# A hybrid decoder layer in float32: where the odd heads' values come back from DRAM, which pool the gates' blocks live in, and which engine multiplies in the gate

## The chip, the core and the metric

The kernel runs on one core of one Trainium2 chip. The engines of a core work side by side: PE (TensorE) multiplies matrices out of on-chip memory (SBUF) into eight accumulator banks (PSUM), ACT (ScalarE) applies functions and copies, DVE (VectorE) does elementwise arithmetic, POOL (GpSimd) and SP (SyncE) here only issue transfers (DMAs). The metric is the device time of one execution in microseconds (us); the median of three runs of the kernel before is 1163.79 us (1162.83 to 1166.5).

## The reference

One layer on 512 tokens, model width 1024, all in float32. What matters here, with the feed-forward part left out:

```python
rq, rk, rv, rg, cq, ckv, krope, gr, gm = jnp.split(rms_norm(x) @ w_in, offsets, axis=-1)
ro = retention(rope(rq), rope(rk), rv)             # 4 heads, q/k width 256, v width 512
a_ret = (rms_norm(ro) * jax.nn.silu(rg)) @ w_br    # head by head, 512 rows of w_br each
a_mla = causal_block_attention(q, k, v) @ w_bm     # 8 heads of latent attention
mixed = jax.nn.sigmoid(gr) * a_ret + jax.nn.sigmoid(gm) * a_mla
x = x + mixed @ w_o
x = x + jnp.square(jax.nn.relu(rms_norm(x) @ w_up)) @ w_down
x = x + jax.nn.sigmoid(rms_norm(x) @ w_ple_gate) * (p @ w_ple)
```

Silu is z times sigmoid(z).

## The kernel before

**Arithmetic.** Activations lie transposed, channels on the 128 partitions and the 512 tokens along the free dimension. Each float32 product is made of three matmuls on a high and a low part of both factors (`mm3`: low by high, high by low, high by high). ACT makes the high part (`wh_...` of a weight), DVE subtracts it from the raw tile for the low part (`wl_...`). A matmul group therefore waits for a chain: DMA, ACT copy, DVE subtraction.

**Products of 2 by 2 blocks in seven parts.** The projections `rv` (values, two heads at a time), `rg` (a head's gate), `br` (a head's rows of w_br) and `dn` (w_down) are each cut into 2 by 2 blocks and made of seven smaller products p = 1, 7, 2, 6, 5, 4, 3. For p = 7, 6 and 4 the weight is a sum of blocks, built in one raw tile: SP loads the first block, and POOL adds the others by accumulating DMAs (L222), for p = 7 at once, for p = 6 only after DVE has taken p = 7's low part out of the tile, for p = 4 only after p = 6's. The raw tile of head h is called `wr_rg{h}70` at all three. The results are joined by `seven_out` (L736): ACT copies p = 1, 7 and 6 out of PSUM into z_11, z_22 and z_21 (L741), DVE adds p = 2, 5 and 4 to them (L746), and p = 3 leaves block 12 in PSUM. PSUM tiles are shared: p = 6 accumulates in the tile of p = 1, so it waits until ACT has copied z_11 away.

**A retention head** h, in PE's order: `ret_qk` (rq, rk), for even h `ret_v` (the values of heads h and h+1), `ret_gate` for p = 1 and 7, `ret_scores` (rs: scores times decay, split into ath and atl), `ret_gate` for p = 2 and 6, `ret_attend` (ro: four groups of 12 matmuls, one for each 128 value channels, and every group goes through all four tiles of values rv{h}0 to rv{h}3), then `ret_gate` for p = 5, 4, 3. The values of the odd heads are stored to DRAM by POOL when they are made (`aside`, L353: v00d to v03d for head 1, v10d to v13d for head 3) and loaded again by SP just before their head (`odd_v`, L779); ACT and DVE split each into rv{h}{j}h and rv{h}{j}l. The gate takes a sigmoid on ACT (L849) and a multiplication by z on DVE (L852). The branch product `br` of head h is done among the next head's rq and rk.

**After the heads**, `ret_turn` (tr) transposes the summed branch for channel block n, `mix` multiplies it by the gate (L943) and adds the attention branch `ze{n}` (L944), and splits it into mix{n}h and mix{n}l. `out_part` starts the first two blocks of the output product `wo` with mix0 to mix3, `out_proj` does the rest.

**Order.** A table of steps (from L1225) is walked at build time. It gives the order of the loads and the order of PE's instructions, which is kept. On ACT, DVE, POOL and SP a list scheduler orders the instructions by its own cost estimates and by the free slots of the tile pools, and each engine then runs its list strictly in that order: an instruction that waits holds up all behind it. The pools that matter: `dyn` with 47 slots for tiles of 128 by 512 (`T`), `keep` with 16 (`K`), six raw weight tiles, three pairs of `wh` and `wl`.

## Time and profile before

| what | us |
|---|---|
| median of three runs (lowest, highest) | 1163.79 (1162.83, 1166.5) |
| the profiled execution: device time | 1163.55 |
| its span, first to last instruction | 1161.8 |
| PE busy | 1110.2 (96%) |
| DVE busy | 783.7 (67%) |
| ACT busy | 548.5 (47%) |
| POOL busy | 85.9 (7%) |
| PE idle, span less busy | 51.6 |
| mean granted PE clock | 0.985 of full |

A row of a timeline reads: start, duration, engine, line, operation, what is written from what is read, partitions by elements, count; in brackets the time the engine stood idle before it, and what ended the wait. A row of issued DMAs reads: destination and source, issuing queue, count, KB each, median us from issue to landing. PE's stages in us of the span, by the first matmuls of each: inputs and attention up to 239.8, its branch product (bm) from there, the retention heads from 283.4, the transposes (tr) from 706.4, the output product (wo) from 715.3, feed-forward (up, dn) from 767.3, embedding (pg) to the end.

### The profile page before, as it was taken

What the parts mean: (1) busy time and instruction counts of PE and PEld (TensorE: products, weight loads), DVE (VectorE), ACT (ScalarE), POOL (GpSimd) and SP (SyncE); (2) the same over time, 40 slices, a digit from 0 to 9 for tenths busy, and PEclk for the clock granted to TensorE, in tenths of its full rate; (3) what the DMA queues carried; (4) which work ended last, traced back from release to release, by engine and by line L of the source; (5) the groups of instructions that cost most, each with busy time, mean ns of one, the idle gap of its engine ahead of it and who ended that gap; (6) DMA issues with size and microseconds to landing.
All of it is one profiled execution on the core that took longest, in us unless ns stands there. A gap on an engine that the chain in (4) does not pass through costs nothing.

```text
span 1161.8 us, 14724 instructions
## 1 busy us (share of the span) xinstructions
PE 1110.2 (96%) x5517; PEld 937.3 (81%) x5517; DVE 783.7 (67%) x1258; ACT 548.5 (47%) x774; POOL 85.9 (7%) x113
## 2 busy tenths in 40 slices
PE   9999989999999989899999698999999999999998
PEld 7878878888889879677878686878888888888877
DVE  7877676557766857866587489554656567567675
ACT  7447556444455535344533453333544344444542
POOL 0000000001120010012000000000100100101000
PEclk9999999999999999999999899999999999999999
DMA  7132222367796774489548663576656755747511
GB/s 258 65 108 88 78 74 64 129 223 221 192 275 163 179 192 113 106 205 259 158 113 201 164 181 111 180 216 200 140 158 191 160 158 179 175 137 193 160 37 73
DMA packets 59799, 182.26 MB, mean 157 GB/s; under 512 B 7312, under 2 KB 8720, under 8 KB 59472
## 3 DMA queue, kind: packets, MB, share of 16 engines
q1 hardware_dynamic: 45744, 131.75, 33.7%
q0 software_dynamic: 13840, 49.55, 22.3%
q8 instruction: 43, 0.70, 0.2%
q14 instruction: 28, 0.23, 0.1%
q10 hardware_dynamic: 144, 0.03, 0.0%
HBM read 167.41 MB, written 11.80 MB: 154 GB/s over the span
## 4 chain that ended last, share of the span: by engine, by line
PE 49%; DMA 7%; DVE 4%; issue 2%; ACT 1%; POOL 0%; SPq 0%; ACTq 0%; POOLq 0%; DVEq 0%
PE up L167 15%; PE dn L167 13%; PE pg L167 4%; PE wo L167 3%; PE rg L167 3%; PE br L167 2%; PE rk L167 2%; DMA wr_rg<-wstream 2%; DMA wr_br<-wstream 2%; PE ro L167 2%; PE gr L167 1%; DMA wr_rv<-wstream 1%; PE rq L167 1%; PE pw L167 1%; DMA v13d<-cv 1%
## 5 line engine op out<-in xcount | busy, mean ns | idle before, releaser
L167 PE MATMUL dn<-wh_dn,cl 128*128 128x512 f32 x224 | 87.2, 389 | 0.0
L167 PE MATMUL dn<-wh_dn,ch 128*128 128x512 f32 x224 | 87.1, 389 | 0.0
L167 PE MATMUL dn<-wl_dn,ch 128*128 128x512 f32 x224 | 87.1, 389 | 0.0
L260 ACT ACTIVATE wh_dn<-wr_dn 128x1024 fp32r<-128x1024 f32 x32 | 34.0, 1063 | 75.7 <-PE up L167 54.3
L260 ACT ACTIVATE wh_up<-wr_up 128x1024 fp32r<-128x1024 f32 x32 | 34.0, 1061 | 58.7 <-PE up L167 29.3
L264 DVE TENSOR_TENSOR wl_dn<-wr_dn,wh_dn 128x1024 fp32r<-128x1024 f32 x32 | 39.1, 1221 | 27.5 <-ACT wh_dn L260 27.5
L260 ACT ACTIVATE wh_rg<-wr_rg 128x1024 fp32r<-128x1024 f32 x28 | 29.4, 1056 | 48.0 <-DMA wr_rg<-wstream 32.8
L264 DVE TENSOR_TENSOR wl_up<-wr_up,wh_up 128x1024 fp32r<-128x1024 f32 x32 | 39.1, 1223 | 18.2 <-ACT wh_up L260 17.9
L1016 DVE SCALAR_TENSOR_TENSOR f<-up,bcx 128x512 f32<-128x512 f32 x32 | 20.6, 686 | 44.1 <-PE up L167 44.1
L167 PEld LDWEIGHTS dn<-wh_dn,cl 128*128 128x128 f32 x224 | 42.1, 188 | 8.8
L167 PEld LDWEIGHTS dn<-wh_dn,ch 128*128 128x128 f32 x224 | 42.1, 188 | 8.7
L167 PEld LDWEIGHTS dn<-wl_dn,ch 128*128 128x128 f32 x224 | 42.1, 188 | 8.6
L260 ACT ACTIVATE wh_rv<-wr_rv 128x1024 fp32r<-128x1024 f32 x28 | 29.6, 1060 | 37.7 <-PE rv L167 11.6
L260 ACT ACTIVATE wh_dn<-dr_dn 128x1024 fp32r<-128x1024 f32 x24 | 25.5, 1061 | 42.5 <-PE up L167 29.4
L264 DVE TENSOR_TENSOR wl_dn<-dr_dn,wh_dn 128x1024 fp32r<-128x1024 f32 x24 | 29.3, 1223 | 22.4 <-ACT wh_dn L260 22.4
L222 POOL DMA_DIRECT2D dr_dn<-wstream x24 | 21.4, 893 | 279.1 <-DMA dr_dn<-wstream 166.0
L260 ACT ACTIVATE wh_br<-wr_br 128x1024 fp32r<-128x1024 f32 x28 | 29.6, 1059 | 25.8 <-DMA wr_br<-wstream 8.9
L264 DVE TENSOR_TENSOR wl_rg<-wr_rg,wh_rg 128x1024 fp32r<-128x1024 f32 x20 | 24.2, 1223 | 25.7 <-ACT wh_rg L260 25.4
L264 DVE TENSOR_TENSOR wl_rv<-wr_rv,wh_rv 128x1024 fp32r<-128x1024 f32 x20 | 24.4, 1224 | 17.4 <-ACT wh_rv L260 15.9
L1074 DVE TENSOR_TENSOR d<-d,dn 128x1024 f32<-128x1024 f32 x24 | 29.3, 1220 | 6.4 <-PE dn L167 6.4
L643 ACT ACTIVATE p<-p,ng,hr 128x128 f32<-128x128 f32 (+3 forms) x32 | 20.6, 647 | 14.9 <-DVE ng L641 14.9
L222 POOL DMA_DIRECT2D wr_br<-wstream x16 | 14.2, 887 | 174.6 <-DVE wl_br L264 53.3
(1917 smaller groups left out, 3669.5 us busy)
## 6 DMA issues: line engine op xcount, KB each, us to landing
wr_up<-wstream SPq DMA_DIRECT2D x32, 512.0 KB, 4.4
wr_dn<-wstream SPq DMA_DIRECT2D x32, 512.0 KB, 3.5
dr_dn<-wstream POOLq DMA_DIRECT2D x24, 512.0 KB, 8.3
wr_rv<-wstream SPq DMA_DIRECT2D x20, 512.0 KB, 4.9
wr_rg<-wstream SPq DMA_DIRECT2D x20, 512.0 KB, 4.7
wr_br<-wstream SPq DMA_DIRECT2D x20, 512.0 KB, 4.9
wr_rv<-wstream POOLq DMA_DIRECT2D x16, 512.0 KB, 7.2
wr_rg<-wstream POOLq DMA_DIRECT2D x16, 512.0 KB, 6.8
```

The costliest lines, as they stand in the source:

```text
L167: return tc.keep_in_program_order(nc.tensor.matmul(*a, **k))
L222: nc.gpsimd.dma_start(raw, chunk(("w", blk, kb, fb, c)), accum_op=ALU.add)
L260: i = ACT(hi, raw, AF.Copy, scale=sign)
L264: TT(lo, raw, hi.bitcast(F32), op=ALU.subtract)
L643: ACT(cols[b], cols[b], AF.Exp, bias=ng[:, b:b + 1], scale=d["rq"][:, b], accum_out=sums[:, b:b + 1])
L1016: STT(u[:, i], ps[:, i], 0.0, V["bcx2"], op0=ALU.max, op1=ALU.mult)
L1074: TT(to, to, dps[p], op=ALU.add if sign > 0 else ALU.subtract)
```

## The change

It has seven parts. (1) `odd_v`'s loads are issued by POOL instead of SP, and the steps move behind `ret_scores`; the low part is written into the loaded tile itself, so a value takes two slots and not three. (2) The gate's p = 7 moves behind `ret_scores`: the gate goes 1, scores, 7, 2, 6. (3) A new ring of four slots `Z` holds the gate's z blocks, the finished `zm` and the half-wise `gr` on their way to DRAM, and block 22 of the values; `dyn` goes from 47 slots to 43. (4) ACT applies Silu in place on z, so the sigmoid tile and DVE's multiplication are gone. (5) Head 0's branch sums `ret` go into the `keep` pool and two other spare tiles, all but one pair. (6) Before the output product, the transposes and mixes of blocks 4 and 5 come behind the first half of wo 0, those of blocks 6 and 7 behind the first half of wo 1; before, all four came ahead of both. (7) In the tail, a broadcast uses the second half of a statistics bank instead of a bank of its own.

```diff
-NDYN, NKEEP, NW, NRAW, NDRAW, AHEAD, PREP, EARLY, PAD = 47, 16, 3, 6, 4, 1, 3, 5, 72
+NDYN, NKEEP, NW, NRAW, NDRAW, AHEAD, PREP, EARLY, PAD = 43, 16, 3, 6, 4, 1, 3, 5, 72
...
+    def Z(name):
+        return dyn.tile([P, S], F32, tag="z", name=name, bufs=4)
...
-            t = T(f"zm{n}")
+            t = Z(f"zm{n}")
...
-            c[to] = T(f"{name}{to}")
+            c[to] = (Z if name[0] == "z" or to == 22 else T)(f"{name}{to}")
...
-            t = T(f"cv{h}{j}")
-            nc.sync.dma_start(t, R[h]["v"][j])
-            R[h]["v"][j] = split(t, f"rv{h}{j}")
+            t = T(f"cv{h}{j}", F32R)
+            nc.gpsimd.dma_start(t.bitcast(F32), R[h]["v"][j])
+            R[h]["v"][j] = split(t.bitcast(F32), f"rv{h}{j}", lo=t)
...
-            sg = T(f"sg{h}{blk}")
-            tc.keep_in_program_order(ACT(sg, z, AF.Sigmoid))
             if blk == 12:
-                d["z"][12] = T(f"z{h}_12")
-            TT(d["z"][blk], z, sg, op=ALU.mult)
+                d["z"][12] = Z(f"z{h}_12")
+            tc.keep_in_program_order(ACT(d["z"][blk], z, AF.Silu))
...
-                ret[b, n] = T(f"ret{b}{n}")
+                if p == 3:
+                    ret[b, n] = keep.tile([P, S], F32, tag=("sum", "bc")[i], name=f"ret{b}{n}", bufs=1)
+                else:
+                    ret[b, n] = (K if p in (1, 7) else T)(f"ret{b}{n}")
...
-        t = T(f"gr{n}")
+        t = (T if half is None else Z)(f"gr{n}")
...
-        pb = bcast(PP("pb" + name)[:, 0], lambda b: V["r" + name][:, b:b + 1])
+        pb = bcast(V["st" + name][:, 1], lambda b: V["r" + name][:, b:b + 1])
...
-        if h % 2:
-            step(None, odd_v, h)
...
-        for p in (1, 7):
-            step(("sw", ("rg", h), p, 0), ret_gate, h, p)
+        step(("sw", ("rg", h), 1, 0), ret_gate, h, 1)
         step(None, ret_scores, h)
-        for p in (2, 6):
+        if h % 2:
+            step(None, odd_v, h)
+        for p in (7, 2, 6):
             step(("sw", ("rg", h), p, 0), ret_gate, h, p)
...
-    for n in range(4, 8):
-        step(None, ret_turn, n)
-        step(None, mix, n)
     for n in range(2):
         step(("o", n), out_part, n, 0)
+        for m in (4 + 2 * n, 5 + 2 * n):
+            step(None, ret_turn, m)
+            step(None, mix, m)
```

The scheduler then places the instructions of four engines anew. Three places follow; of the rows' line numbers, those of the change are a few higher (L226 is the accumulating DMA, L264 the weight's high part, L268 its low part, L745 the z copy).

**Head 3's gate, POOL's queue.** Of `wr_rg370` the first row shown is the accumulation for p = 6, the second that for p = 4. Before:

```order
L222 DMA wr_rg350_6040<-wstream 128x1024
L222 DMA wr_rg370_5943<-wstream 128x1024
L222 DMA wr_br370_6345<-wstream 128x1024
L222 DMA wr_rg370_5943<-wstream 128x1024
L222 DMA wr_br350_6505<-wstream 128x1024
```

Now:

```order
L226 DMA wr_rg370_5915<-wstream 128x1024
L226 DMA wr_br370_6307<-wstream 128x1024
L784 DMA cv30_6030<-v10d_5238 128x512
L226 DMA wr_rg370_5915<-wstream 128x1024
L784 DMA cv31_6035<-v11d_5242 128x512
L784 DMA cv32_6040<-v12d_5148 128x512
L784 DMA cv33_6045<-v13d_5151 128x512
L226 DMA wr_br350_6465<-wstream 128x1024
```

One value's load stands ahead of the accumulation for p = 4, three behind it; in head 1 it is two ahead and two behind.

**The same place on ACT** (`z_..<-rg` are the copies out of PSUM, `ath` the splits of the scores, `wh_rg_..<-wr_rg_5943` and `..5915` the weights of p = 6 and p = 4 from the shared tile). Before:

```order
L305 ACTIVATE rv32h<-cv_5992 128x512
L305 ACTIVATE rv33h<-cv_5998 128x512
L260 ACTIVATE wh_rg_6251<-wr_rg_5943 128x1024
L741 ACTIVATE z_11_6034<-rg_6009 128x512
L741 ACTIVATE z_22_6068<-rg_6043 128x512
L305 ACTIVATE ath<-s_6079 128x512
L305 ACTIVATE ath<-s_6090 128x384
L305 ACTIVATE ath<-s_6101 128x256
```

Now:

```order
L264 ACTIVATE wh_rg_6050<-wr_rg_5936 128x1024
L745 ACTIVATE z_11_5982<-rg_5957 128x512
L309 ACTIVATE ath<-s_5993 128x512
L309 ACTIVATE ath<-s_6004 128x384
L264 ACTIVATE wh_rg_6084<-wr_rg_5915 128x1024
```

```order
L264 ACTIVATE wh_rg_6116<-wr_rg_6054 128x1024
L309 ACTIVATE rv30h<-cv_6030 128x512
L264 ACTIVATE wh_rg_6217<-wr_rg_5915 128x1024
L855 ACTIVATE z_11_5982<-z_11_5982 128x512
L309 ACTIVATE rv31h<-cv_6035 128x512
L745 ACTIVATE z_21_6146<-rg_5957 128x512
L264 ACTIVATE wh_rg_6269<-wr_rg_6120 128x1024
L309 ACTIVATE rv32h<-cv_6040 128x512
L309 ACTIVATE rv33h<-cv_6045 128x512
```

Before, the z copies came behind the values and behind p = 4's weight. Now z_11 comes ahead of both p = 6's and p = 4's weight, and the splits of three of the four values come behind p = 4's weight.

**The output product, DVE** (`ge` and `gr` are the gates that become mix4 to mix7, `wl_o` low parts of w_o). Before:

```order
L943 TENSOR_TENSOR gr_6533<-tr_6751,gr_6533 128x512
L306 TENSOR_TENSOR mix4l<-ge_6408,mix4h 128x512
L944 TENSOR_TENSOR gr_6533<-gr_6533,ze_6412 128x512
L306 TENSOR_TENSOR mix5l<-gr_6445,mix5h 128x512
L943 TENSOR_TENSOR gr_6726<-tr_6762,gr_6726 128x512
L306 TENSOR_TENSOR mix6l<-gr_6533,mix6h 128x512
L944 TENSOR_TENSOR gr_6726<-gr_6726,ze_6414 128x512
L264 TENSOR_TENSOR wl_o_6776<-wr_o_6773,wh_o_6775 128x1024
L306 TENSOR_TENSOR mix7l<-gr_6726,mix7h 128x512
```

Now:

```order
L951 TENSOR_TENSOR ge_6364<-ge_6364,ze_6362 128x512
L268 TENSOR_TENSOR wl_o_6691<-wr_o_6688,wh_o_6690 128x1024
L310 TENSOR_TENSOR mix3l<-ge_6364,mix3h 128x512
L268 TENSOR_TENSOR wl_o_6733<-wr_o_6730,wh_o_6732 128x1024
L950 TENSOR_TENSOR ge_6368<-tr_6707,ge_6368 128x512
L950 TENSOR_TENSOR gr_6405<-tr_6719,gr_6405 128x512
```

The second and third `wl_o` stand ahead of everything that mix4 to mix7 need, the second ahead of mix3's low part too.

**The attention's first pair of heads, DVE** (`ha`, `hr`, `nt` are the steps to the heads' normalising factor, which PE's broadcast `pbk` reads; `tra`, `trk` a table of angles for the retention heads). Before:

```order
L604 TENSOR_TENSOR hr<-hr,f_464 128x16
L605 TENSOR_SCALAR nsc<-hr 128x8
L264 TENSOR_TENSOR wl_kq_1034<-wr_kq_1031,wh_kq_1033 128x640
L678 TENSOR_TENSOR zm_946<-gm_915,rbc 128x512
L468 TENSOR_SCALAR tra<-posf,cst 128x512
L264 TENSOR_TENSOR wl_gm_0_1069<-wr_gm_0_1066,wh_gm_0_1068 128x512
L469 TENSOR_SCALAR trk<-tra 128x512
```

Now:

```order
L474 TENSOR_SCALAR trk<-trk 128x512
L328 TENSOR_SCALAR hr<-ha 128x16
L481 SCALAR_TENSOR_TENSOR tra<-trk,tra 128x512
L329 TENSOR_SCALAR hr<-hr 128x16
L481 SCALAR_TENSOR_TENSOR tra<-trk,tra 128x512
L331 TENSOR_TENSOR nt_895<-hr 128x16
L481 SCALAR_TENSOR_TENSOR tra<-trk,tra 128x512
L332 SCALAR_TENSOR_TENSOR nt_895<-nt_895,ha 128x16
L481 SCALAR_TENSOR_TENSOR tra<-trk,tra 128x512
```

The angles were made behind `hr`; now they are made between its steps.

Elsewhere POOL has 125 instructions for 117, SP 333 for 341, DVE 1244 for 1260, ACT two more, both loads of a function table; PE's instructions are the same in kind and number.

4 lines of the change are left out of this document (3 added, 1 removed).

## The prediction

> **What bounds the kernel now.** I read the busy times of the page first, then who waited for whom on PE, then the stages, then the timelines at the long waits.
>
> ```profile
> PE 1110.2 (96%) x5517; PEld 937.3 (81%) x5517; DVE 783.7 (67%) x1258; ACT 548.5 (47%) x774; POOL 85.9 (7%) x113
> ```
>
> PE is the bound, and its work does not change. Only its idle time, 1161.8 of span less 1110.2, 51.6 us, and what it loses to a slower clock can move. The waits of PE, with their sum, count and longest:
>
> ```profile
> PE rg L167 <- ACT z L741: 17.4, 3, 9.9
> PE rk L167 <- DVE wl_rk L264: 5.8, 2, 3.1
> PE wo L167 <- DVE wl_o L264: 4.6, 1, 4.6
> PE pbk L167 <- DVE hr L604: 3.1, 2, 2.3
> ```
>
> The first and the third are what the change touches. Two stretches (length, then busy time and count of PE, PEld, DVE, ACT, POOL, then the granted clock) show that a long wait costs more than itself:
>
> ```profile
> 420.00:440.00 20.00, 13.61 (x92) 13.15 (x92) 9.49 (x14) 7.58 (x12) 1.72 (x2) 0.85 0.76 200
> ...
> 630.00:660.00 30.00, 20.05 (x134) 18.95 (x135) 14.54 (x21) 10.40 (x18) 2.61 (x3) 0.83 0.68 170
> ```
>
> The clock is 0.85 and 0.83 around the two longest waits, where its mean over the span is 0.985. The waits themselves, in heads 1 and 3, at p = 6 of the gate, and the shorter one of head 2:
>
> ```profile
> 436.50 0.58 PE L167 MATMUL rg<-s60h,wl_rg 128*128 128x256 f32 x1 [6.39 <-ACT z L741]
> 652.79 0.58 PE L167 MATMUL rg<-s60h,wl_rg 128*128 128x256 f32 x1 [9.88 <-ACT z L741]
> 560.97 0.38 PE L167 MATMUL rg<-s60h,wl_rg 128*128 128x256 f32 x1 [1.17 <-ACT z L741]
> ```
>
> ACT's z copies are late because ACT goes in order and is stuck on something else. Head 1, then head 3, each with the last copy of ro:
>
> ```profile
> 433.87 0.63 ACT L305 ACTIVATE rv12h<-cv 128x512 fp32r<-128x512 f32 x1 [7.30 <-DMA cv<-v02d]
> ...
> 449.30 0.69 ACT L819 ACTIVATE og<-ro,gn 128x512 f32<-128x512 f32 x1 [0.75 <-PE ro L167]
> ...
> 651.20 1.06 ACT L260 ACTIVATE wh_rg<-wr_rg 128x1024 fp32r<-128x1024 f32 x1 [7.70 <-DMA wr_rg<-wstream]
> 652.16 1.07 ACT L741 ACTIVATE z<-rg 128x512 f32<-128x512 f32 x2
> ...
> 661.72 0.69 ACT L819 ACTIVATE og<-ro,gn 128x512 f32<-128x512 f32 x1 [0.75 <-PE ro L167]
> 665.58 0.69 ACT L819 ACTIVATE og<-ro,gn 128x512 f32<-128x512 f32 x1 [0.75 <-PE ro L167]
> ```
>
> In head 1 it is a value's load, in head 3 the weight of p = 4. The last two rows give the length of ro: two groups end 3.86 us apart, so a group takes 1.93 us. ACT waits for the last group and takes it at once, so ro ends at 449.3 and 665.5.
>
> **The gate's p = 6.** Now z_11 stands ahead of everything slow, so p = 6 starts when PE gets there: 436.50 - 6.39 = 430.1 and 652.79 - 9.88 = 642.9. Both waits go as such. Next late are the values. Ro comes right behind p = 6 in PE's order, each of its groups reads all four values, and the last ones are loaded by POOL behind the accumulation for p = 4. POOL's issues (head 0, where two value stores stand right behind an accumulation, then the accumulations for p = 4 in heads 1 and 3), and times from issue to landing:
>
> ```profile
> 345.37 0.88 POOL L222 DMA_DIRECT2D wr_rg<-wstream  x1 [4.86 <-DVE wl_rg L264]
> 345.94 0.88 POOL L353 DMA_DIRECT2D v00d<-cv  x1
> 346.51 0.88 POOL L353 DMA_DIRECT2D v01d<-cv  x1
> ...
> 426.65 0.86 POOL L222 DMA_DIRECT2D wr_rg<-wstream  x1 [7.95 <-DVE wl_rg L264]
> ...
> 643.89 0.89 POOL L222 DMA_DIRECT2D wr_rg<-wstream  x1 [1.94 <-issue]
> ```
>
> ```profile
> wr_rg<-wstream POOLq DMA_DIRECT2D x1, 512.0 KB, 6.8
> v00d<-cv POOLq DMA_DIRECT2D x1, 256.0 KB, 7.6
> v01d<-cv POOLq DMA_DIRECT2D x1, 256.0 KB, 8.2
> wr_rg<-wstream POOLq DMA_DIRECT2D x1, 512.0 KB, 5.6
> v11d<-cv POOLq DMA_DIRECT2D x1, 256.0 KB, 2.3
> ```
>
> The first three land at 352.2, 353.5 and 354.7: 256 KB behind an accumulation lands 1.3 and 2.5 us after it, a third, I take it, 3.8. Alone it takes 2.3 (v11d). These are stores; the trace shows no load on POOL that isn't a weight.
>
> *Head 3.* The accumulation was issued at 643.89 when DVE had p = 6's low part, and that is no earlier now; it landed at 651.2, when ACT went on. Behind it on ACT stand its weight (1.06), the silu (0.6), rv31h, z_21, another weight, rv32h and rv33h: with steps of 1.0 for a weight and 0.5 for a tile 4.7 us, then DVE's low part 0.7, so the fourth value is complete at 656.6 (by landing alone, 651.2 + 3.8 + 0.6 + 0.7 = 656.3). The first group of ro ends 0.4 later, the other three take 5.8: 662.8. PE has then stood from about 648 with little to do, and I add 1.0 for the clock: 663.8 against 665.5, **-1.7**.
>
> *Head 1.* The accumulation for p = 4 is now behind p = 7 and the scores on DVE: by the order p = 7's low part comes after four more DVE operations, about 2.4 us, and p = 6's after three splits of scores as well, so I put the issue at 430.4 instead of 426.65. With the same 5.6 it lands at 436.0. Only two values are behind it: weight, rv12h, z_21, weight, rv13h 3.6 us, low part 0.7, 440.3; ro ends at 440.3 + 0.4 + 5.8 + 1.0 = 447.5. Before, ro ended at 449.3: **-1.8**. (There, 449.3 less four groups of 1.93 leaves 5.1 us for p = 6 from 436.50, 24 matmuls at the slow clock.)
>
> Bounds for each: 2.5 better, with no loss of clock (1.0) and a landing 1.5 sooner (head 3's accumulation took 7.3, head 1's 5.6, and v11d needed only 2.3); 2.6 worse, with the last value two steps of 1.3 later.
>
> *Head 2* has no values to bring back. Its z copy was held by the slot of v11d's store, and z now has its own ring: **-1.0** of the 1.17, bounds -1.2 and 0.
>
> A rule speaks to the price. The Trainium skill, "DMA: Bandwidth & Descriptors", section "Anatomy of one DMA", fits a transfer issued by GpSimd as 2.0 us plus bytes over 436 GB/s, 3.2 us for 512 KB; by it the accumulations would land at 433.6 and 647.1, and both heads would gain some 2.4 and 4.1 us more. The accumulations of this trace, 5.6 and 6.8, are against it.
>
> **The output product.** PE and DVE before:
>
> ```profile
> 713.63 1.91 PE L167 MATMUL tr<-cst,ret 128*128 128x128 f32 x16
> 715.30 0.48 PE L167 MATMUL wo<-mix0h,wl_o 128*128 128x512 f32 x1
> ...
> 717.89 0.39 PE L167 MATMUL wo<-mix3h,wh_o 128*128 128x512 f32 x1
> 722.88 0.76 PE L167 MATMUL wo<-mix0h,wl_o 128*128 128x512 f32 x1 [4.60 <-DVE wl_o L264]
> ...
> 733.15 0.39 PE L167 MATMUL wo<-mix7h,wh_o 128*128 128x512 f32 x1
> ```
>
> ```profile
> 714.27 0.69 DVE L943 TENSOR_TENSOR ge<-tr,ge 128x512 f32<-128x512 f32 x1
> 721.51 1.22 DVE L264 TENSOR_TENSOR wl_o<-wr_o,wh_o 128x1024 fp32r<-128x1024 f32 x1
> ```
>
> Twelve matmuls take 2.6 + 0.2 = 2.8 us. The 36 from 722.88 on end at 733.4, 10.5 us where 8.4 would do: the slow clock took 2.1. DVE had twelve operations of 0.6 us between the first row and the awaited weight. Now the weight stands ahead of them, ready near 715.4, before PE asks. PE goes 12 (716.4), two transposes (half of 1.67, 717.3), 12 (720.1), two transposes (720.9), 24. Of these, mix6 needs four DVE operations on the turned blocks and its low part: 5 by 0.6 after 720.9, 723.9, while PE wants it 6 matmuls in, 722.5. So a new wait of 1.4, and 720.9 + 5.6 + 1.4 = 727.9 against 733.4: **-5.5**, bounds -6.9 (no wait) and -3.4 (the wait also costs 2.1 of clock).
>
> The Trainium skill, "TensorE: Matmul & The Clock Gate", Part 1, says that the array falls to half clock after an idle window of about 3.4 us and needs about 3.4 us of work to return; by it the new wait here costs no clock, and the new waits in heads 1 and 3, over 3.4 us, cost 1.7 each where I took 1.0.
>
> **The attention's first heads.** The order shows the angle table between the steps to `hr`:
>
> ```profile
> 80.60 0.17 DVE L600 TENSOR_TENSOR ha<-st,f 128x16 f32<-128x16 f32 x1
> ...
> 83.63 0.18 DVE L604 TENSOR_TENSOR hr<-hr,f 128x16 f32<-128x16 f32 x1
> ...
> 85.94 0.48 DVE L468 TENSOR_SCALAR tra<-posf,cst 128x512 f32<-128x512 f32 x1
> 86.94 0.42 DVE L469 TENSOR_SCALAR trk<-tra 128x512 f32<-128x512 f32 x1
> ...
> 87.85 2.87 DVE L477 SCALAR_TENSOR_TENSOR tra<-trk,tra 128x512 f32<-128x512 f32 x4
> ...
> 85.14 1.03 PE L167 MATMUL pbk<-cst,hr 128*128 128x128 f32 x8
> ```
>
> Eight such operations, 2.87 + 0.48 + three of 0.42, 4.6 us, now come ahead of hr, of which perhaps 1 us hides in the gaps of a chain that took 3.2 for fifteen tiny operations. Hr was ready at 83.8 and is now at about 87.4; PE asks at 85.14 and waits some 2.3 us. DVE is free sooner afterwards, and later waits of that head may shrink. I take **+1.0**; bounds -1 (all comes back) and +4.6.
>
> **At nothing.** The gate's multiplications leave DVE:
>
> ```profile
> L852 DVE TENSOR_TENSOR z<-z,sg 128x512 f32<-128x512 f32 x12 | 8.2, 686 | 0.4 <-ACT sg L849 0.4
> ```
>
> Sixteen of them, 11 us, lie beside PE's gate and branch matmuls; uncovered they would be worth up to 0.7 each at p = 3. Two more table loads lie on ACT, 47% busy. SP loses eight issues, and the tail's broadcast waits for the same statistics as before. Of the shorter pool the order shows one late load: the first four `ze` now come only after head 3's p = 6, still 60 us ahead of the mixes around 714.27. The waits of rk (5.8) keep their chain.
>
> **Sum.** -1.7 - 1.8 - 1.0 - 5.5 + 1.0 = -9.0; from the profiled 1163.55 that is 1154.55, and since that execution lies 0.24 under the median, **1154.8**.
>
> **Rivals.** (a) *The values come in time.* v11d's 2.3 speaks for it, v00d and v01d behind an accumulation against. With the early bounds of both heads, 2.5 each: 1154.8 - 5.0 = 1149.8, and 1147 if wo also waits for nothing and the angles cost less. By the skill's fit of a transfer, above, both heads' 6.5 would make it 1148.3. (b) *The stall only changes its name:* the values land a further 2.6 late in both heads, wo meets the slow clock (+2.1), head 2 keeps its wait (+1.0): 1154.8 + 8.3 = 1163.1, no change. The 7.70 us that ACT stood at p = 4's weight in head 3 show what an accumulation can hold up; against it speaks that the values issued at 345 landed in order, close behind theirs. (c) *Slower: the angle table and the shorter pool in the attention.* If what delays hr once delays each of the four pairs of heads, four waits of 2.3, with the 2.1 of clock that wo's wait of 4.6 brought, cost 4 by 4.4 = 17.6, net of the 1.0 already counted 16.6: 1171.4. It decides from 12.5 us of such loss on, and against it speaks that only the first pair's order shows the angles.
>
> **Chances.** Forecast 0.58 (1152 to 1159), (a) 0.15, (b) 0.15, (c) 0.12. Faster needs under 1160.3 (0.3%, what a measurement can tell): 0.55 of the forecast's, all of (a), a little of (b): 0.72; the same 0.16, slower 0.12. The range that leaves a tenth on each side: 1147 to 1166.
>
> **What would show it.** Right: p = 6 of heads 1 and 3 without a wait at 430 and 643, ro waiting there for rv12 and rv31 or later values, ro's end 1 to 3 us earlier; wo's second group without a wait and a short one at mix6; pbk waiting about 2 us for hr. Wrong: values landing with or before p = 4's accumulation, or waits of several us in the attention.

## The result, and the profile after

The kernel changed takes 1158.05 us (median of six runs, 1155.28 to 1160.51) beside 1163.99 us of the kernel before on the same chip (six runs): a ratio of 0.9946 [0.9924, 0.9967], 5.9 us less. The forecast was 1154.8. Its profiled execution took 1160.51 us with a span of 1158.4, so its rows show where time moved, and their sum, 3.0 us less, understates the gain by 2.9.

The busy times after the change, then the waits of PE (sum, count, longest):

```profile
PE 1112.1 (96%) x5517; PEld 936.8 (81%) x5517; DVE 772.6 (67%) x1242; ACT 551.3 (48%) x776; POOL 90.3 (8%) x121
```

```profile
PE ro L167 <- DVE cv L310: 11.9, 4, 4.7
PE sqr L167 <- DVE mx L641: 9.7, 1, 9.7
PE pbk L167 <- DVE hr L608: 2.7, 3, 1.4
PE br L167 <- ACT bx33h L309: 2.2, 1, 2.2
PE rk L167 <- DVE wl_rk L268: 1.7, 2, 0.9
PE rg L167 <- DVE wl_rg L268: 1.5, 1, 1.5
...
PE wo L167 <- ACT mix6h L309: 1.0, 1, 1.0
```

The gate's waits for z, 17.4 us, are gone, and so are most of wo's and of rk's. Two new ones stand at the head of the list: `ro` waits for the values, which the prediction had, and `sqr`, in the attention, waits 9.7 us in one piece, which it had not. Reading the start of the same PE instruction in the profiles shows where the time went. Each column is the difference from the kernel before, in us; the columns behind "after" are experiments 11, 3, 2, 1, 10 and 12 of the next section. A column is one execution: those of "after", experiment 3, 2 and 1 lay 2.5, 3.9, 2.8 and 4.4 us above their kernels' medians, that of experiment 10 lay 2.0 below, so a difference of 2 or 3 us that stands in one column alone may be of that execution:

```
                              before   after  reorder    Silu      wo   spare  earliest   tiles
                                                alone   alone   alone   tiles    values    only
rq of head 0                  283.37  +10.75   +0.03   -0.06  +1.20   +4.10    +3.92   +4.45
gate p = 1 of head 1          417.43  +12.00   -0.01   +2.61  +1.20   +5.65    +3.87   +4.41
gate p = 5 of head 1, past ro 449.10  +12.18   +5.64   +3.10  +0.87   +7.65    -3.32   -2.55
gate p = 1 of head 2          546.31   +8.49   +2.82   -0.29  +0.25   +2.05    -8.91   -7.35
gate p = 5 of head 2, past ro 573.16   +4.74   -0.93   +0.34  +2.18   -1.70   -12.66  -11.10
gate p = 1 of head 3          629.96   +1.22   -0.72   -3.14  +0.62   -5.23   -16.18  -14.62
gate p = 5 of head 3, past ro 665.38   +0.26   -2.50   -0.31  +2.64   -6.50   -26.61  -25.58
first transpose (tr)          706.43   +3.01   -2.32   +2.49  +2.93   -1.93   -23.93  -22.52
feed-forward (up)             767.28   -3.03   -4.38   +2.95  -3.14   -8.01   -29.99  -28.60
```

The attention, with its branch product, lost 10.75 us. The rest of the kernel gained 13.8, more than the 10 of the terms after it, and at other places than the prediction put them.

**The wait of 9.7 us.** DVE of the changed kernel at that place, then the queue of SP (the first two rows, the last copy out of `qr11h`, and the last two), then PE:

```profile
152.71 0.69 DVE L310 TENSOR_TENSOR qr11l<-o,qr11h 128x512 fp32r<-128x512 f32 x1 [0.49 <-ACT qr11h L309]
...
154.06 0.68 DVE L310 TENSOR_TENSOR qr21l<-o,qr21h 128x512 fp32r<-128x512 f32 x1
162.47 0.29 DVE L641 CUSTOM_DVE_ANT_0 p<-sc,kf 128x128 f32<-128x128 f32 x1 [7.74 <-DMA qp<-qr11h]
```

```profile
152.70 0.51 SPq L572 DMA_DIRECT2D qp<-qr11h  x1
153.27 0.58 SPq L572 DMA_DIRECT2D qp<-qr21h  x1
...
160.44 0.53 SPq L572 DMA_DIRECT2D qp<-qr11h  x1
...
161.65 0.59 SPq L572 DMA_DIRECT2D qp<-qr11l  x1
162.28 0.59 SPq L572 DMA_DIRECT2D qp<-qr21l  x1
```

```profile
162.92 1.41 PE L167 MATMUL sqr<-cst,sa 128*128 128x4 f32 x6 [9.66 <-DVE mx L641]
```

DVE stands 7.74 us before a softmax tile `p`, on a copy of a query part `qr`. The copies into `qp` are sixteen, of 64 KB each, issued 0.64 us apart from 152.70 to 162.28 and landing 2 us later each; the last one out of `qr11h`, issued at 160.44, landed at about 162.4, and DVE went on at 162.47. The softmax tiles take the slots of `dyn` in which the `qr` parts lie, and a slot is free only when all copies out of it have landed. With 47 slots, it seems, there had been others; no run has the rest of the change with a larger pool. In the kernel before, the same softmax operation came at once:

```profile
150.78 0.69 DVE L306 TENSOR_TENSOR qr21l<-o,qr21h 128x512 fp32r<-128x512 f32 x1
151.39 0.29 DVE L637 CUSTOM_DVE_ANT_0 p<-sc,kf 128x128 f32<-128x128 f32 x1
```

**The values.** ACT in head 1 and head 3 after the change, with the last copies of ro:

```profile
447.56 1.06 ACT L264 ACTIVATE wh_rg<-wr_rg 128x1024 fp32r<-128x1024 f32 x1 [2.90 <-DMA wr_rg<-wstream]
449.27 0.63 ACT L309 ACTIVATE rv12h<-cv 128x512 fp32r<-128x512 f32 x1 [0.65 <-DMA cv<-v02d]
...
451.23 0.62 ACT L309 ACTIVATE rv13h<-cv 128x512 fp32r<-128x512 f32 x1
...
461.48 0.69 ACT L824 ACTIVATE og<-ro,gn 128x512 f32<-128x512 f32 x1 [0.75 <-PE ro L167]
...
651.19 1.06 ACT L264 ACTIVATE wh_rg<-wr_rg 128x1024 fp32r<-128x1024 f32 x1 [3.47 <-DMA wr_rg<-wstream]
...
655.15 0.63 ACT L309 ACTIVATE rv33h<-cv 128x512 fp32r<-128x512 f32 x1
...
665.84 0.69 ACT L824 ACTIVATE og<-ro,gn 128x512 f32<-128x512 f32 x1 [0.75 <-PE ro L167]
```

Both heads follow the prediction's mechanism: p = 6 no longer waits for z, and the splits rv12 and later stand on ACT behind the weight of p = 4, for whose accumulation ACT stands 2.90 and 3.47 us. PE's waits there, and then three stretches (length, busy time and count of five engines, granted clock, share of the transfer engines, GB/s):

```profile
450.67 0.58 PE L167 MATMUL ro<-ath,cv 128*128 128x256 f32 x1 [4.47 <-DVE cv L310]
453.24 0.58 PE L167 MATMUL ro<-ath,cv 128*128 128x256 f32 x1 [1.56 <-DVE cv L310]
...
654.16 0.69 PE L167 MATMUL ro<-ath,cv 128*128 128x384 f32 x1 [4.70 <-DVE cv L310]
656.63 0.58 PE L167 MATMUL ro<-ath,cv 128*128 128x256 f32 x1 [1.14 <-DVE cv L310]
```

```profile
440.00:460.00 20.00, 13.97 (x81) 12.72 (x80) 9.63 (x13) 9.41 (x15) 2.90 (x4) 0.83 0.59 158
640.00:660.00 20.00, 12.65 (x76) 11.07 (x75) 8.67 (x11) 9.50 (x15) 3.40 (x6) 0.79 0.87 246
150.00:175.00 25.00, 15.34 (x76) 13.29 (x75) 13.40 (x49) 9.88 (x23) 0.00 (x0) 0.73 0.20 52
```

The clock is 0.83 and 0.79, as low as around the waits that were removed, and 0.73 around the new wait in the attention, where the kernel before has 0.93 in the same stretch.

### The profile page after: what moved, and what is told of

It reads as the page before. It is cut to its first block, busy times and chain, and to the rows that moved or that the text cites. A ratio compares the mean times of both kernels' runs of the same rounds, so it can differ in the third digit from the quotient of the medians.

```text
span 1158.4 us, 14701 instructions
## 1 busy us (share of the span) xinstructions
PE 1112.1 (96%) x5517; PEld 936.8 (81%) x5517; DVE 772.6 (67%) x1242; ACT 551.3 (48%) x776; POOL 90.3 (8%) x121
## 4 chain that ended last, share of the span: by engine, by line
PE 81%; DMA 7%; DVE 6%; ACT 3%; issue 3%; SPq 1%; POOL 0%; ACTq 0%; POOLq 0%; DVEq 0%
PE up L167 15%; PE dn L167 13%; PE rv L167 5%; PE rg L167 4%; PE pg L167 4%; PE rq L167 4%; PE bm L167 4%; PE gr L167 4%; PE br L167 4%; DMA wr_rg<-wstream 3%; PE wo L167 3%; PE gm L167 3%; PE rk L167 3%; PE sc L167 3%; PE ro L167 2%
## 5 line engine op out<-in xcount | busy, mean ns | idle before, releaser
L264 ACT ACTIVATE wh_dn<-wr_dn 128x1024 fp32r<-128x1024 f32 x32 | 34.0, 1062 | 75.4 <-PE up L167 54.3
L264 ACT ACTIVATE wh_up<-wr_up 128x1024 fp32r<-128x1024 f32 x32 | 34.0, 1061 | 56.6 <-PE up L167 29.3
L268 DVE TENSOR_TENSOR wl_dn<-wr_dn,wh_dn 128x1024 fp32r<-128x1024 f32 x32 | 39.1, 1221 | 27.5 <-ACT wh_dn L264 27.5
L268 DVE TENSOR_TENSOR wl_up<-wr_up,wh_up 128x1024 fp32r<-128x1024 f32 x32 | 39.1, 1222 | 17.7 <-ACT wh_up L264 17.2
L264 ACT ACTIVATE wh_rg<-wr_rg 128x1024 fp32r<-128x1024 f32 x28 | 29.6, 1056 | 42.5 <-DMA wr_rg<-wstream 30.3
L264 ACT ACTIVATE wh_rv<-wr_rv 128x1024 fp32r<-128x1024 f32 x28 | 29.6, 1059 | 38.7 <-PE rv L167 13.9
L264 ACT ACTIVATE wh_br<-wr_br 128x1024 fp32r<-128x1024 f32 x28 | 29.6, 1059 | 35.6 <-issue 12.6
L264 ACT ACTIVATE wh_dn<-dr_dn 128x1024 fp32r<-128x1024 f32 x24 | 25.5, 1061 | 41.0 <-PE up L167 28.2
L268 DVE TENSOR_TENSOR wl_dn<-dr_dn,wh_dn 128x1024 fp32r<-128x1024 f32 x24 | 29.3, 1222 | 22.1 <-ACT wh_dn L264 22.1
L226 POOL DMA_DIRECT2D dr_dn<-wstream x24 | 21.4, 903 | 272.7 <-DVE wl_dn L268 119.7
L268 DVE TENSOR_TENSOR wl_rg<-wr_rg,wh_rg 128x1024 fp32r<-128x1024 f32 x20 | 24.3, 1222 | 25.4 <-ACT wh_rg L264 25.3
L268 DVE TENSOR_TENSOR wl_rv<-wr_rv,wh_rv 128x1024 fp32r<-128x1024 f32 x20 | 24.4, 1222 | 15.2 <-ACT wh_rv L264 15.0
L268 DVE TENSOR_TENSOR wl_br<-wr_br,wh_br 128x1024 fp32r<-128x1024 f32 x20 | 24.3, 1217 | 3.4 <-ACT wh_br L264 3.4
```

The source lines that it names most:

```text
L226: nc.gpsimd.dma_start(raw, chunk(("w", blk, kb, fb, c)), accum_op=ALU.add)
L264: i = ACT(hi, raw, AF.Copy, scale=sign)
L268: TT(lo, raw, hi.bitcast(F32), op=ALU.subtract)
```

## The experiments

All were timed beside the kernel before, which had medians of 1164.84, 1163.37, 1163.29 and 1163.63 us beside experiments 1 to 4, 5 to 8, 9 to 11 and 12. Kernels of different groups are compared by their ratios to it.

**1. The two high parts out of `dyn`.** Is the wait of 9.7 us one of slots?

```diff
-        h1, l1 = split(o1, f"qr1{gq}")
-        h2, l2 = split(o2, f"qr2{gq}")
+        h1, l1 = split(o1, f"qr1{gq}", hi=spare("sum", f"qr1{gq}h"))
+        h2, l2 = split(o2, f"qr2{gq}", hi=spare("bc", f"qr2{gq}h"))
```

`spare` takes the tiles "sum" and "bc" of `keep`, unused at that time.

> The changed kernel with one difference: the high parts of the attention's rotary queries (qr1, qr2) lie in two tiles of the keep pool that stand empty until the retention heads, so that no softmax tile has to take their slots. Theory: in the changed kernel PE's 9.66 us at 162.9 come from head 3's softmax, whose tiles p30 and p32 lie in the slots of qr11h and qr21h and wait until SP has copied these out (DVE stood 7.74 for that copy). Then the wait falls under 1.5, the first rq, 10.7 us late against the kernel before, is at most 2 us late, and the time is 1158.05 - 9 = about 1149 (1147 to 1151). Rival: the softmax is late for another reason (scores, angles, stats), or the next tile runs into the same shortage: wait of 5 or more left somewhere in the attention, time 1155 or above.

1150.85 us, ratio 0.9882 [0.986, 0.9903]: 7.4 us less than the change (0.9946 against 0.9882 of 1164). PE's waits in the attention, profile of this kernel:

```profile
PE pbk L167 <- DVE hr L611: 4.4, 4, 2.0
...
PE st L167 <- ACT sums L596: 2.8, 2, 1.4
PE sqr L167 <- DVE mx L644: 1.8, 1, 1.8
```

The one wait fell from 9.7 to 1.8, and the attention's loss from 10.75 to 4.10 (table), where the theory had under 1.5 and at most 2. So 6.6 us of it were the slots of the `qr` parts. What is left is spread over waits of 1.1 to 2.0 around the angle table and the softmax; it was not taken apart further.

**2. The output product alone**, part 6 of the change on the kernel before:

```diff
-    for n in range(4, 8):
-        step(None, ret_turn, n)
-        step(None, mix, n)
     for n in range(2):
         step(("o", n), out_part, n, 0)
+        for m in (4 + 2 * n, 5 + 2 * n):
+            step(None, ret_turn, m)
+            step(None, mix, m)
```

> The kernel before with part 6 alone: transposes and mixes of blocks 4 to 7 between the first halves of wo 0 and wo 1. Theory, as in the prediction: the wait of 4.60 for wl_o and its slow clock go, a wait of about 1 to 1.4 at mix6 comes: -5.5 (-4.5 to -6.5), 1158.5. Rival: the gain needs the other parts (the freer DVE), and here mix4 to mix7 come later: -3 or less.

1157.2 us, ratio 0.9937 [0.9917, 0.9957], 7.3 us less than before, 5.0 to 9.7 by the interval. In the table this kernel falls from +2.93 at the transposes to -3.14 at the feed-forward: 6.1. All else stayed as before, the waits for z and of rk too. By the medians the whole change was worth less than this part of it, though the two intervals overlap.

**3. Silu alone**, part 4 on the kernel before:

```diff
-            sg = T(f"sg{h}{blk}")
-            tc.keep_in_program_order(ACT(sg, z, AF.Sigmoid))
...
-            TT(d["z"][blk], z, sg, op=ALU.mult)
+            tc.keep_in_program_order(ACT(d["z"][blk], z, AF.Silu))
```

> The kernel before with part 4 alone: Silu on ACT in place of sigmoid and DVE's multiplication. In the changed kernel the waits of rk for its low part (3.07 and 2.76) are down to 0.86 and 0.87, which the prediction had left as they were. Theory: DVE, free of the multiplications, has the branch weight of p = 7 split sooner, POOL's accumulation for p = 6 starts sooner, and ACT, which holds rk's chain up while it waits for that weight, is free sooner: here too rk's two waits fall under 1.5, and the time falls by 4 to 7 (1157 to 1160). Rival: the rk waits fell because of the new gate order or the z ring: here they stay near 3, and the time changes by 1 at most.

1162.42 us, ratio 0.9983 [0.9968, 0.9999]: 2.0 us less, where 4 to 7 were expected. The waits of rk did fall from 3.1 and 2.8 to 0.9 each, but the table shows +2.61 after head 0 and 2.8 lost again between head 3 and the transposes. Experiments 8 and 9 show what goes with Silu there.

**4. Values by SP at the late place**, on the kernel of experiment 1: `nc.gpsimd.dma_start` for `cv` becomes `nc.sync.dma_start`.

> The kernel of e1 with the odd heads' values loaded by SP instead of POOL, at the same step behind the scores. Theory: ro's waits in heads 1 and 3 (4.47 + 1.56 and 4.70 + 1.14 in the changed kernel) come from values that stand behind the accumulation for p = 4 in POOL's queue and behind its weight on ACT; over SP they land some 4 to 6 us after their issue, beside the accumulation, but ACT's order still puts two or three of them behind that weight: 2 to 5 us less than e1. Rival: the price is in ACT's order alone, or SP's own queue holds them up: the waits stay, the time is e1's within 1.

1150.3 us, ratio 0.9883 [0.9862, 0.9903]: the same as experiment 1. ACT of this kernel in head 3:

```profile
641.14 1.06 ACT L264 ACTIVATE wh_rg<-wr_rg 128x1024 fp32r<-128x1024 f32 x1 [5.35 <-DMA wr_rg<-wstream]
```

Two of the values had been asked for at 626.08 and 626.55, and the split of the second, rv31h, still stood behind this weight. The other two SP asked for only at 637.51 and 639.79, after it had stood 10.0 us for a weight's tile, and rv33h waited 1.26 for its load. So another queue gains nothing at this place; that the order on ACT, and not a queue, holds the values is clear from rv31h here, and for all of them only from the next two experiments. The Trainium skill, "DMA: Bandwidth & Descriptors", section "Issuing engines are not separate DMA queues", says that all issuers end up on the same sixteen engines, and another issuer only saves the time to issue. The two ratios, 0.9882 and 0.9883, don't speak against it, but with the splits behind ACT's order they can't test it.

**5 and 6. Values one step earlier**, ahead of the gate's p = 1 and of the scores, by POOL and by SP, on the kernel of experiment 1:

```diff
+        if h % 2:
+            step(None, odd_v, h)
         step(("sw", ("rg", h), 1, 0), ret_gate, h, 1)
         step(None, ret_scores, h)
-        if h % 2:
-            step(None, odd_v, h)
         for p in (7, 2, 6):
```

> The kernel with the two high parts in spare tiles (1150.85 us), and the odd heads' values asked for one step earlier, ahead of the gate's p = 1 and of the scores, still by POOL. On ACT the four splits of the values then stand ahead of the weight of p = 4, where before three or four of them stood behind it. Theory (ACT's order behind the weight of p = 4 makes ro wait, not the transfers of the values): the waits of ro for cv (5.5 + 1.6 in head 1, 0.9 + 4.2 + 1.1 in head 3, 13.2 in all) go, p = 6 of the gate stays without a long wait, and of 13.2 some 8 to 10 come back, since the weight of p = 4 itself is late and PE asks for it earlier: 1141 to 1144. Rival one (POOL's queue: two loads ahead of each accumulation make those 2 to 4 us later): waits of 2 to 4 us appear at p = 6 or at p = 4 in both heads, 1147 to 1151. Rival two (whatever stands on ACT, the transfers land late): ro keeps its waits, 1150 to 1152.

> As the run before, but the values' loads issued by SP at the earlier step, so that POOL's accumulations have nothing new ahead of them. Theory (order on ACT): the waits of ro go as well, 1141 to 1144, and 0 to 3 us less than with POOL's queue if its loads delay the accumulations there. Rival (SP's queue, where the loads stand behind weights that wait for their tiles): the values land late, ACT stands at them with p = 1's copy behind, and p = 6 waits as it did before the change, several us in both heads: 1150 to 1156.

1143.74 us, ratio 0.9828 [0.9814, 0.9841], and 1142.78 us, ratio 0.9823 [0.9803, 0.9842]: 6 to 7 us less than experiment 1. The times are in the theory's range, the gain is a little under its 8 to 10. `ro` waits for no value any more. What it waits for next, in the profile of the kernel with POOL's loads:

```profile
641.44 1.06 ACT L264 ACTIVATE wh_rg<-wr_rg 128x1024 fp32r<-128x1024 f32 x1 [7.98 <-DMA wr_rg<-wstream]
642.40 0.40 ACT L309 ACTIVATE ath<-s 128x256 fp32r<-128x256 f32 x1
```

```profile
642.86 0.58 PE L167 MATMUL ro<-ath,cv 128*128 128x256 f32 x1 [7.36 <-ACT ath L309]
```

The same weight of p = 4 still holds ACT, now for 7.98 us, and the operation caught behind it is the last of the scores' splits. With POOL's loads the accumulation was issued at 632.00 and ACT went on at 641.44; with SP's it was issued at 634.60 and ACT went on at 639.93, and the wait is 3.1. The two totals don't differ by what can be told. The loads were late on neither queue. The rival of later accumulations fell in the total only: with POOL's loads this one took 9.4 us to land instead of 5.3 and landed 1.5 us later, issued 0.57 us behind another of 512 KB (631.43).

**7. The gate's p = 7 ahead of the scores again**, on the kernel of experiment 1, one part of the reordering undone:

```diff
         step(("sw", ("rg", h), 1, 0), ret_gate, h, 1)
+        step(("sw", ("rg", h), 7, 0), ret_gate, h, 7)
         step(None, ret_scores, h)
...
-        for p in (7, 2, 6):
+        for p in (2, 6):
```

> The kernel with the two high parts in spare tiles (1150.85 us), and the gate's p = 7 back ahead of the scores, as before the change; the values stay behind the scores, on POOL. This undoes one part of the reordering alone. By the order all four splits of a value then stand behind the weight of p = 4 on ACT, in head 1 as in head 3. Theory (order on ACT): p = 6 waits for nothing, ro's wait in head 1 grows by the two more splits, 2 to 3 us, head 3 stays, and POOL's accumulation for p = 4 is asked for some 3 us earlier in both heads, which gives 2 to 4 of it back: 1149 to 1153. Rival (p = 7 behind the scores is what costs the rest, since it delays the accumulations): 1144 to 1148.

1158.47 us, ratio 0.9959 [0.9946, 0.9973]: 9 us more than experiment 1, where the theory had no loss and the rival a gain. PE's waits of this kernel:

```profile
PE ro L167 <- DVE cv L310: 17.9, 6, 6.0
```

Against 13.2 in experiment 1. The direction was the theory's (four splits behind the weight of p = 4 in head 1 instead of two), the return of 2 to 4 us from an earlier accumulation did not come, and the waits explain 4.7 of the 9. PE is 4.4 us later than in experiment 1 already at p = 1 of head 1's gate, ahead of these waits; why was not taken apart.

**8 and 9. Silu taken back**, on the kernels of experiments 1 and 6:

```diff
+            sg = T(f"sg{h}{blk}")
+            tc.keep_in_program_order(ACT(sg, z, AF.Sigmoid))
+            TT(d["z"][blk], z, sg, op=ALU.mult)
-            tc.keep_in_program_order(ACT(d["z"][blk], z, AF.Silu))
```

> The kernel with the two high parts in spare tiles (1150.85 us), with the Silu of the gate taken back: a sigmoid into a tile of its own on ACT and a multiplication on DVE, 16 more operations of 0.69 us on DVE. Theory (the shorter wait of rk and the gain in head 2 come from the Silu): rk waits about 3.0 and 2.8 again instead of 0.9 twice, and the end is 4 to 6 us later: 1155 to 1157. Rival (the time that rk gets is given back at the next weight that was accumulated, as in the run with the Silu alone, where the total moved 2 us): rk waits longer but the next wait shrinks, 1151 to 1153.

> The kernel with the values asked for early on SP (1142.78 us), with the gate's Silu taken back to a sigmoid and a multiplication. Theory (the Silu's two table loads on ACT, at the start of its use in head 0 and at the sigmoid of the token gate behind head 3, are each in front of something that PE waits for: so in head 0 by 1.4, and br for bx33h by 1.5 more than for its rival on DVE): 1139 to 1141, so is not waited for and the last br waits 1.3. Rival (the 2.6 us of the run without Silu were noise or an accident of the order): 1142 to 1144.

1148.26 us, ratio 0.9873 [0.986, 0.9887], about 1 us under experiment 1 and not to be told from it; and 1138.81 us, ratio 0.9783 [0.9764, 0.9801], 4.7 us under experiment 6, as the theory of experiment 9 had it. The theory of experiment 8 fell whole, and its rival's time was missed too: rk still waits 0.9 twice without Silu. Why, shows DVE around the branch weight of p = 7, whose low part POOL awaits before the accumulation for p = 6. First the kernel before, then experiment 8, DVE and POOL of each:

```profile
466.33 1.43 DVE L904 SCALAR_TENSOR_TENSOR ret<-br,nro,ret 128x512 f32<-128x512 f32 x2
...
468.28 2.35 DVE L264 TENSOR_TENSOR wl_br<-wr_br,wh_br 128x1024 fp32r<-128x1024 f32 x2
```

```profile
470.03 0.86 POOL L222 DMA_DIRECT2D wr_br<-wstream  x1 [10.63 <-issue]
```

```profile
471.02 1.22 DVE L268 TENSOR_TENSOR wl_br<-wr_br,wh_br 128x1024 fp32r<-128x1024 f32 x1
472.15 1.40 DVE L916 SCALAR_TENSOR_TENSOR ret<-br,nro,ret 128x512 f32<-128x512 f32 x2
```

```profile
472.53 0.86 POOL L226 DMA_DIRECT2D wr_br<-wstream  x1 [7.57 <-DVE wl_br L268]
```

In the kernel before, the weight's low part stands on DVE behind two branch sums and a split; in experiment 8 it stands ahead of them, and the same after the change and with Silu alone. POOL issues 8.4 us after its last accumulation instead of 11.5, and the 2.43 us that ACT stood for that weight before (477.44) go. The scheduler's order decides it: Silu moves it, and so does some other part of the change without Silu, but not the reordering alone (experiment 11: 5.7 for rk) nor the output product alone. Experiment 12 narrows it to the tiles.

Silu's cost is on ACT. The rows of experiment 1, in head 0 and behind head 3:

```profile
366.69 1.28 ACT L858 ACT_TABLE_LOAD   x1
...
670.68 1.28 ACT L952 ACT_TABLE_LOAD   x1
```

Neither is in a kernel without Silu, and neither is PE's wait for `sqo` in head 0 (1.28 at 375.09 in experiment 1): all seven kernels with Silu have it, of 0.25 to 1.37, and none of the seven without. From the first rq to head 1's gate those with Silu lose 0.5 to 4.5 us against the kernel before, those without nothing (0.05 at most). Behind head 3 it is less clear. The last `br`, which waited 2.81 for bx33h in experiment 1, waits 1.32 and 1.26 in experiments 8 and 9, but experiments 10 and 12, also without Silu, lose 2.7 and 3.1 us between head 3's ro and the transposes, as much as the change does. So the cost in head 0 goes with Silu; how much of the second is the table's load and how much the order was not taken apart.

**10. Values earlier still**, ahead of the second half of the key's projection, on the kernel of experiment 9:

```diff
-            branch_steps(h - 1, [1, qk("rq", 1), 7, 2, qk("rk", 0), 6, 5, qk("rk", 1), 3, 4])
+            early = [lambda h=h: step(None, odd_v, h)] if h % 2 else []
+            branch_steps(h - 1, [1, qk("rq", 1), 7, 2, qk("rk", 0), 6, 5, qk("rk", 1), *early, 3, 4])
```

The step ahead of the gate goes.

> The run before (early values on SP, no Silu) with the values asked for one step earlier still, ahead of the second half of the key's projection. By the order three or four of the turned scores' splits (ath) then stand ahead of the weight of p = 4 on ACT instead of one to three. Theory (what ro still waits for, ath, 1.6 in head 1 and 3.1 in head 3, is again ACT's order behind that weight): 3 to 4 us less than the run before. Rival (the accumulation itself sets the end, and PE only waits at p = 6 or p = 4 instead): within 1.5 us of the run before.

1135.16 us (1132.95 to 1137.72), ratio 0.9751 [0.973, 0.9772]: 3.7 us less again, as the theory had it. It beats both the kernel before, by 2.5%, and the change, by 2.0%. ACT and PE of this kernel in head 3:

```profile
630.15 1.26 ACT L309 ACTIVATE ath<-s 128x384 fp32r<-128x384 f32 x3
634.74 1.06 ACT L264 ACTIVATE wh_rg<-wr_rg 128x1024 fp32r<-128x1024 f32 x1 [3.33 <-DMA wr_rg<-wstream]
```

```profile
PE ro L167 <- ACT ath L309: 0.8, 1, 0.8
```

All splits of the scores are ahead of the weight of p = 4. ACT still stands 3.33 us there, and nobody waits for what is behind it.

**11. The reordering alone**, parts 1 and 2 on the kernel before: values on POOL behind the scores, p = 7 behind the scores.

```diff
-            nc.sync.dma_start(t, R[h]["v"][j])
+            nc.gpsimd.dma_start(t.bitcast(F32), R[h]["v"][j])
...
-        if h % 2:
-            step(None, odd_v, h)
...
-        for p in (1, 7):
-            step(("sw", ("rg", h), p, 0), ret_gate, h, p)
+        step(("sw", ("rg", h), 1, 0), ret_gate, h, 1)
         step(None, ret_scores, h)
-        for p in (2, 6):
+        if h % 2:
+            step(None, odd_v, h)
+        for p in (7, 2, 6):
```

> The kernel before with one part of the change alone: odd heads' values behind the scores and on POOL, gate's p = 7 behind the scores; no tiles of their own for the gate, no Silu, no shorter pool, the output product as before. By the order all four splits of the values stand behind the weight of p = 4 on ACT in both heads, and the copy for p = 7 behind them. Theory (order on ACT): the gate's waits of 17.4 us go, and ro waits 16 to 18 for the values in their place: 1161 to 1166. Rival (the prediction's terms, 1.7 and 1.8 less): 1159 to 1161.

1159.7 us, ratio 0.9965 [0.9952, 0.9978], 4.1 us less than before. PE's waits of this kernel:

```profile
PE ro L167 <- DVE cv L306: 17.2, 7, 7.9
PE rk L167 <- DVE wl_rk L264: 5.7, 2, 3.1
PE wo L167 <- DVE wl_o L264: 4.6, 1, 4.6
```

The time is the rival's, the mechanism the theory's: 17.4 us of waits for z became 17.2 of waits for values. By the table, head 1 lost 5.6 and head 3 gained 1.8; the total comes from head 2 (-3.7), from the projections ahead of it (-2.8) and from the output product (-2.1), whose wait is the same 4.6. The longest wait has another reason than the theory's: POOL issued the fourth value's load only at 436.45, behind the accumulation for a branch weight (435.88), and ACT stood for it 9.46 us.

**12. The tiles of their own, without the reordering.** The kernel of experiment 8 with parts 1 and 2 undone: `cv` loaded by SP at its old place (its low part still written into the loaded tile), the gate's p = 1 and 7 ahead of the scores.

```diff
+        if h % 2:
+            step(None, odd_v, h)
         for p in (1, 7, 2, 6, 5, 4, 3) if h % 2 == 0 else ():
...
-        step(("sw", ("rg", h), 1, 0), ret_gate, h, 1)
+        for p in (1, 7):
+            step(("sw", ("rg", h), p, 0), ret_gate, h, p)
         step(None, ret_scores, h)
-        if h % 2:
-            step(None, odd_v, h)
-        for p in (7, 2, 6):
+        for p in (2, 6):
```

> The kernel with spare tiles and without Silu, with the reordering of the odd heads undone as well: left of the change are the tiles of their own for the gate, the branch sums in spare tiles, the output product and the tail's bank. By the order the branch weight's low part for p = 7 stands ahead of the two branch sums on DVE, as after the change. Theory (the tiles of their own move that place, and with it the wait of rk): rk waits 0.9 twice instead of 3.1 and 2.8, the gate's waits for z stay near 17, wo waits 1.0; with 7 us from rk, 6 to 7 from wo and 4 lost in the attention 1152 to 1156. Rival (rk's wait needs the reordering or the Silu as well): rk waits about 3 twice, 1159 to 1162.

1134.61 us (1133.73 to 1135.4), ratio 0.9749 [0.9736, 0.9762]: 14 us less than experiment 8, as fast as experiment 10, and 17 us under the lower end of what I expected. The part on rk held: 0.9 twice, so the tiles of their own move that weight's place without Silu and without the reordering. But "the gate's waits for z stay near 17" fell: no wait for z is left. ACT of this kernel in head 3:

```profile
616.55 0.63 ACT L309 ACTIVATE rv30h<-cv 128x512 fp32r<-128x512 f32 x1 [0.94 <-DMA cv<-v10d]
618.50 0.60 ACT L748 ACTIVATE z<-rg 128x512 f32<-128x512 f32 x1 [1.32 <-PE rg L167]
...
626.63 2.01 ACT L264 ACTIVATE wh_rg<-wr_rg 128x1024 fp32r<-128x1024 f32 x2 [3.23 <-DMA wr_rg<-wstream]
```

In the kernel before both z copies of this head stood behind the weight of p = 4 (652.16); here, with the values and the gate in their old order, z_11 stands ahead of all the slow weights, and PE does not wait at p = 6. The changes of tiles (the ring for z, head 0's sums and the `qr` parts elsewhere, two slots for a value) were enough to have it scheduled there; which of them was not tried.

This kernel and that of experiment 9 differ in one thing, the place of the gate's p = 7; the values stand at the old place in both. So of the 14 us that the reordering cost, some 10 lie in the values behind the scores (0.9873 to 0.9783, experiments 8 and 9; the loads' other queue changed little in experiments 4 and 6) and some 4 in the later p = 7 (0.9783 to 0.9749): in head 3 of experiment 9 the last split of the scores stands behind the weight of p = 4, here all four stand ahead of it, and ro's waits for these splits are 5.3 us there and 1.0 here. Experiment 10 gets as much with the later p = 7 by asking for the values earlier still.

## Why the prediction was right, and where it was wrong

The total was near (1158.05 against 1154.8, inside 1152 to 1159), but that is luck in part: an error of 10 us in the attention was set off by gains that the sum did not hold.

- **The attention, +1.0: the step that failed.** The angle table cost what was said: `pbk` waited 1.44 for `hr`, and PE was 1.4 late there. But "of the shorter pool the order shows one late load" was wrong. The shortage of slots cost 6.6 us at another place (experiment 1), and some 2.7 more went in small waits whose cause stays open. I had looked for instructions that moved; a slot taken by a later tile changes the wait of an instruction that stays where it is. Rival (c) had the pool and the attention, and nearly the size from which it decides (10.75 against 12.5), but another mechanism.
- **The gate's p = 6: whose gain it is.** I put the end of the waits for z to the reordering as much as to the ring of four slots, and named the ring only for head 2. Experiment 12 has the tiles without the reordering: no wait for z, and 14 us less than with both, 10 of them from the place of the values and 4 from that of p = 7. The reordering traded 17.4 us of waits for z, which the tiles remove anyway, for 11.9 of waits for values.
- **Head 3, -1.7, measured -1.0; head 1, -1.8, measured +0.2.** The mechanism was right in each step. In head 1, whose start lies 12.0 later, the accumulation landed at 435.6, counted in the times of the kernel before (436.0 predicted), and PE's last wait for a value ended at 441.2 (440.3 predicted). In head 3, 1.2 later, these are 650.0 (651.2) and 655.4 (656.6). The mis-sized term is the clock. From the last wait's end to the last copy of ro it took 8.2 and 9.2 us (453.24 to 461.48, 656.63 to 665.84) where the sum had 0.4 + 5.8 + 1.0 = 7.2. In just these stretches the clock was 0.76 and 0.71, and PE waited for nothing; in the same ro of the kernel before it was 1.00. So it cost 2.0 and 3.0, not 1.0. The 1.7 worked out from the Trainium skill, "TensorE: Matmul & The Clock Gate", Part 1, was nearer, if still low.
- **Head 2, -1.0, measured -3.7.** The 1.17 for z was one of three waits there; two more were in the trace of the kernel before:

```profile
549.89 0.39 PE L167 MATMUL rg<-s70h,wl_rg 128*128 128x256 f32 x1 [0.55 <-DVE wl_rg L264]
...
567.04 0.39 PE L167 MATMUL ro<-atl,rv1211h 128*128 128x256 f32 x1 [0.91 <-DVE atl L306]
```

  All three are gone. The reordering alone brings the same 3.7 (-0.93 less +2.82), and so do the tiles alone (-11.10 less -7.35); Silu alone does not. The kernel with the reordering alone has no ring, so the ring that I named is one way to end this wait and not the only one.
- **The output product, -5.5: right.** -6.1 in the profiles, -7.3 with 2.4 either way in time, alone. The wait at mix6 was 1.0 where 1.4 was said, and the clock stayed at full there, as the window in Part 1 of that page of the Trainium skill has it for a wait that short.
- **Costed at nothing, and not nothing.** "The waits of rk keep their chain": they fell from 5.8 to 1.7, and by the table the stretches from head 1's to head 2's gate and from head 2's to head 3's brought 3.7 and 3.5. The chain is the one that I named; what I took for fixed was the place of one weight's low part in DVE's order. "Two more table loads lie on ACT, 47% busy": a share of busy time says nothing about the moment, and the first load stands 8 us ahead of a wait of PE (so, 1.0) that only the kernels with Silu have. Between head 3 and the transposes the change lost 2.8; how much of that is the second load stays open.
- **The rivals.** (a), the values in time, did not happen. (b), the stall only changes its name, is what the reordering alone did to the waits of heads 1 and 3 together (16.3 us for z became 17.2 for values), though not in the total.

## What to carry to other kernels

When a pool is made smaller, ask for every tile that now takes an older tile's slot who still reads the old one, transfers out of it above all: the instruction that pays need not have moved. On an engine that runs in strict order, put what is ready ahead of the operation that stands for a late transfer; here the late weight could stay late (3.3 us on ACT in experiment 10) once everything PE needed was ahead of it. And time the parts alone, and the whole without each: of this change the output product brought 7 us, the new places of tiles took away the waits for z and rk, the shortage of slots cost 7 by one stall, and the reordering, needless beside the tiles, cost 14.

## What the runs showed of the hardware

- Sixteen copies of 64 KB on one queue left 0.64 us apart and landed 2.0 us after their issue, so a tile that the first and the thirteenth of them read (qr11h) was held from 152.70 to about 162.4, while the transfer engines were busy to a mean share of 0.20.
- An accumulation of 512 KB took 5.4 us (442.20 to 447.56) and 5.5 (645.71 to 651.19) to land, and 9.4 in head 3 of experiment 5 (632.00 to 641.44), where another was issued 0.57 us before it. The fit of the Trainium skill, "DMA: Bandwidth & Descriptors", section "Anatomy of one DMA", which the prediction quoted with 3.2 us, doesn't hold for it in these kernels.
- Two waits of 4.5 and 4.7 us and the short ones behind them cost 2 and 3 us more by the slower clock (0.76 and 0.71 behind them); the wait of 1.0 at wo cost none (1.00 from 715 to 733).
